# Stick-breaking attention in a hybrid decoder layer: queries on partitions, a scan for the running product, DMA transposes for the weights

## The chip, the cores and the metric

The kernel runs on one core of a Trainium2 chip. The metric is device time of one execution in microseconds (us), taken as the median of three runs. The profile is one further execution; its engines are PE (TensorE matmul; PEld is its weight load), DVE (VectorE), ACT (ScalarE), POOL (GpSimd) and SP (SyncE, which issues most DMAs).

## The reference

One layer: normalise x, project, attend, convolve, gate, project back, and then a feed-forward block with a convolution inside. What the change touches is the attention, with 8 heads of 64 and 1024 positions:

```python
z = jnp.einsum("bhqd,bhkd->bhqk", qb, kb).astype(jnp.float32) * scale
strict = s_idx < t_idx
log_keep = jnp.where(strict, jax.nn.log_sigmoid(-z), 0.0)
later = lax.cumsum(log_keep, axis=3, reverse=True) - log_keep
w = jnp.where(strict, jnp.exp(jax.nn.log_sigmoid(z) + later), 0.0)
outs.append(jnp.einsum("bhqk,bhkd->bhqd", w, vb.astype(jnp.float32)))
```

In words: beta = sigmoid(z). The weight of key s for query t is beta[t,s] times the product of (1 - beta[t,j]) over the keys j between s and t. It is strictly causal. The product can be taken as an exponential of a sum of logarithms, or as a running product that starts at the newest key and runs back.

## The kernel before

Every float32 matrix product is made of three float16 ones: each operand is kept as a high and a low half, and `PASSES` (L35) names the three pairs of halves that are multiplied. A high half is written by an ACT copy, and the low half by a DVE instruction that subtracts the high half from the source. Weights arrive by DMA from SP into `ws` tiles (L103), are squared and summed by ACT (L56), scaled by a power of two and split into `wh` tiles (L86, L87).

The mixer begins with the normalisation of x and the first projections, in an order written out by hand. Then come four calls of `attention(j)`, each for a **pair of heads** (the two heads of a pair lie on partitions 0 to 63 and 64 to 127 of the tiles q and k). Beside each call the function `merge` runs a stream of **projection matmuls**: v for the later positions, q and k of the next pair (`qk_tile`, L200), the convolution branch (`pcc`, `pcx`, `pcb`), and, with the last pair, gates and the first branch outputs. These fill PE while a unit of the attention waits for DVE and ACT. `merge` only sets an order in the source; the final order on each engine is made by a scheduler at build time from dependences and priorities, and is then fixed: each engine takes its instructions in that order and waits when an operand isn't ready.

A pair is cut into twelve **units**. Before the change a unit is one tile of 128 keys (on partitions) by up to 512 queries; widths are 128, 256, 384 and 512, twice each, and 512 four times more, 4608 columns per head in all. The steps of a unit:

- z (L600, six matmuls, three passes for two heads) in PSUM; one buffer of two banks.
- zc: DVE scales z and clamps it, with a mask tile `clamp` on diagonal units (L615, L618).
- sp: ACT takes exp and then ln(1 + .), the softplus (L622, L623); its high half by ACT (L625), its low half by DVE (L626).
- A: PE multiplies sp with a triangle of ones (L600, four matmuls) to sum over the later keys, and after it was read with the other triangle (four more), so that A carries the sum on to the next unit. A takes two banks.
- zc minus A on DVE (L638), exp on ACT (L640): the weights w, with keys on partitions. High half by ACT (L642), low half by DVE (L643).
- o: PE multiplies w with v (L600, six matmuls as wide as the unit, with 64 columns of v as the stationary operand).

All these matmuls are issued by the helper `mm`, so that they have one line, L600. The step o of a unit is written two units after its z.

After the mixer come the branch products (L580), the gates and the out-projection (L859), and the feed-forward block (L1156 and L1048), which the change leaves alone.

Of the kernel before, what the change touches and what calls it, by code (L numbers as in the profile page):

```python
# [37 lines left out]
class Layer:  # L38
# [167 lines left out]
    def build(self):  # L206
# [23 lines left out]
        with ExitStack() as top:  # L230
# [9 lines left out]
            nc.scalar.preload_act_table_set("natural_log_exp_and_others")  # L240
# [7 lines left out]
            self.one = c.tile([P, 1], F32, tag="one", name="one")  # L248
            nc.vector.memset(self.one, 1.0)
            self.cmw = c.tile([P, 4, 3], F32, tag="cmw", name="cmw")  # L250
            self.cfw = c.tile([P, 2 * NFF, 3], F32, tag="cfw", name="cfw")
            tri32 = c.tile([P, P], F32, tag="tri32", name="tri32")
            nc.gpsimd.memset(tri32, 1.0)
            nc.gpsimd.affine_select(tri32, tri32, [[-1, P]], ALU.is_ge, 0.0, base=0, channel_multiplier=1)
            self.tri = c.tile([P, 2, P], F16, tag="tri", name="tri")
            nc.vector.tensor_copy(self.tri[:, 0, :], tri32)
            nc.vector.tensor_scalar(self.tri[:, 1, :], tri32, -1.0, 1.0, ALU.mult, ALU.add)
# [6 lines left out]
    def mixer(self, mid):  # L264
        tc, nc, a = self.tc, self.nc, self.a
        hT = self.hp.tile([P, 2, KD, T], F16, tag="hT", name="hT")
        with ExitStack() as ph1:
# [4 lines left out]
            self.clamp = att.tile([P, 2, NH], F16, tag="clamp", name="clamp")  # L272
            nc.gpsimd.memset(self.clamp, 44.0)
            nc.gpsimd.affine_select(self.clamp[:, :, :P], self.clamp[:, :, :P], [[0, 2], [1, P]], ALU.is_gt,
                                    -30000.0, base=0, channel_multiplier=-1)
# [4 lines left out]
            def qk_tile(j, which):  # L280
# [12 lines left out]
                if which == "k":  # L293
                    cz = self.small(f"cz{j}", keep=True)
                    self.mul(cz[:, 0:1], s["iq"], inv)
                    self.mul(cz[:, 1:2], cz[:, 0:1], cst[:, 0:1])
                    s["cz"] = cz[:, 1:2]
# [293 lines left out]
            def attention(j):  # L591
# [3 lines left out]
                units = [dict(c=c, i=i, off=max(0, i * P - c * NH), top=i == 4 * c + 3, diag=i >= 4 * c,  # L595
                              nm=f"{j}_{c}{i}") for c in range(2) for i in range(4 * c + 3, -1, -1)]
# [5 lines left out]
                def stage1(u):  # L602
                    off, i, c, nm = u["off"], u["i"], u["c"], u["nm"]
                    tsl = ds(c * NH + off, NH - off)
                    z = pat.tile([P, 2, NH], F32, tag="z", name=f"z{nm}")
                    for n, (hk, hq) in enumerate(PASSES):
                        for h in range(2):
                            d = ds(64 * h, 64)
                            with tc.high_priority(10 ** 6):
# [676 lines left out]
```

## Time and profile before

| what | value |
|---|---|
| median of 3 runs | 1367.35 us (1366.69 to 1368.55) |
| profiled execution | 1367.47 us |
| its span, first to last instruction | 1365.7 us |
| PE busy in the span | 1336.1 us |
| DVE busy | 1028.6 us |
| ACT busy | 860.7 us |
| attention stage, first z to last o | about 64 to 411 us |
| moved by DMA | 96.06 MB |

The profiled execution's own time lies 1.8 us above its span. A row of the profile that ends in "x48 | 45.7, 955 | 34.5 <-ACT w L642 34.4" is a group of 48 instructions that were busy for 45.7 us, with a mean of 955 ns; the engine sat idle for 34.5 us just before them, 34.4 of these until an ACT instruction on tile w was done.

### The profile page before, as it was taken

To read this page: it belongs to the slowest core of one execution; us is meant where nothing else is said; L and a number is where in the kernel's file an instruction comes from. 1 tells how busy PE (TensorE), PEld (TensorE's weight loads), DVE (VectorE), ACT (ScalarE), POOL (GpSimd) and SP (SyncE) were. 2 spreads that over 40 slices of the span, in tenths; PEclk is the share of its full clock that TensorE was granted. 3 is DMA by queue.
4 is the path that set the end of the run, shared out by engine and by line. 5 is a ranking of instruction groups with operands and counts; after the bars stand their busy time and mean duration, and the time that the engine had idled before them with its cause. 6 is when DMAs were issued, how large, how long until landed. Compare 5 with 4: busy or idle time off the path is not lost. (4 is left out here: it accounts for less than half of the span.)

```text
span 1365.7 us, 16990 instructions
## 1 busy us (share of the span) xinstructions
PE 1336.1 (98%) x6651; PEld 607.7 (44%) x6651; DVE 1028.6 (75%) x1610; ACT 860.7 (63%) x1204; POOL 34.2 (3%) x52
## 2 busy tenths in 40 slices
PE   6999999999999999999999999999999999999997
PEld 3444444444444444444454444444444444444443
DVE  6667777777775965878788985984894896699855
ACT  6668778787775775666466577652761673476524
POOL 2000000000000000000010000000000000000002
PEclk9999999999999999999999999999999999999999
DMA  7102111101111121351331123122220321313216
GB/s 264 62 1 62 32 31 32 38 25 39 40 31 47 32 62 31 93 185 36 119 124 62 62 62 123 39 87 85 70 78 16 123 62 62 109 45 124 63 46 109
DMA packets 26576, 96.06 MB, mean 70 GB/s; under 512 B 3072, under 2 KB 3200, under 8 KB 26496
## 3 DMA queue, kind: packets, MB, share of 16 engines
q1 hardware_dynamic: 25056, 89.74, 20.3%
q0 software_dynamic: 1440, 5.24, 2.1%
q8 instruction: 52, 0.85, 0.2%
q14 instruction: 28, 0.23, 0.1%
HBM read 86.58 MB, written 8.39 MB: 70 GB/s over the span
## 5 line engine op out<-in xcount | busy, mean ns | idle before, releaser
L1156 PEld LDWEIGHTS <-wh_u 128*128 128x128 f16 x1848 | 178.8, 98 | 217.3 <-issue 3.5
L1048 PE MATMUL pd<-wdh,f 128*128 128x512 f16 (+1 forms) x1068 | 230.3, 377 | 2.8 <-ACT wdh L86 1.2
L1048 PEld LDWEIGHTS <-f 128*128 128x128 f16 x1068 | 104.4, 98 | 127.2 <-issue 4.3
L86 ACT ACTIVATE wh_u<-ws_u,sc 128x1024 f16<-128x1024 f32 (+1 forms) x66 | 64.7, 998 | 102.9 <-DVE sc L78 79.3
L1055 DVE SCALAR_TENSOR_TENSOR yacc<-pd,sd,yacc 128x512 f32<-128x512 f32 (+1 forms) x81 | 58.5, 740 | 72.7 <-PE pd L1048 65.2
L1156 PEld LDWEIGHTS <-wh_g 128*128 128x128 f16 x588 | 56.9, 98 | 68.7 <-issue 0.4
L859 PE MATMUL py<-wh_wo,m 128*128 128x512 f16 x384 | 83.9, 379 | 0.0
L87 DVE SCALAR_TENSOR_TENSOR wh_u<-ws_u,sc,wh_u 128x1024 f16<-128x1024 f32 (+1 forms) x66 | 72.1, 1099 | 9.5 <-ACT wh_u L86 9.4
L643 DVE SCALAR_TENSOR_TENSOR w<-zc,w 128x1024 f16<-128x1024 f32 (+3 forms) x48 | 45.7, 955 | 34.5 <-ACT w L642 34.4
L622 ACT ACTIVATE sp<-zc 128x1024 f32<-128x1024 f32 (+3 forms) x48 | 40.2, 838 | 46.7 <-DVE zc L615 29.1
L600 PE MATMUL A<-sh,tri 128*128 128x512 f16 (+3 forms) x352 | 67.8, 322 | 0.0
L1233 DVE SCALAR_TENSOR_TENSOR ugu<-cgu,cw_g,ugu 128x1023 f32<-128x1023 f32 (+1 forms) x44 | 56.2, 1278 | 11.3 <-ACT ugu L1231 10.9
L1233 DVE SCALAR_TENSOR_TENSOR ua<-cau,cw_a,ua 128x1023 f32<-128x1023 f32 (+1 forms) x44 | 56.1, 1276 | 1.4 <-ACT ua L1231 1.3
L859 PEld LDWEIGHTS <-m 128*128 128x128 f16 x384 | 37.5, 98 | 44.1
L626 DVE TENSOR_TENSOR sh<-sp,sh 128x1024 f16<-128x1024 f32 (+3 forms) x48 | 45.7, 952 | 12.9 <-ACT sh L625 12.7
L640 ACT ACTIVATE zc<-zc 128x1024 f32<-128x1024 f32 (+3 forms) x48 | 40.0, 834 | 15.4 <-DVE zc L638 15.0
L638 DVE SCALAR_TENSOR_TENSOR zc<-A,zc 128x1024 f32<-128x1024 f32 (+3 forms) x48 | 45.5, 949 | 2.3 <-PE A L600 2.3
L56 ACT ACTIVATE jk_u<-ws_u 128x1024 bf16<-128x1024 f32 x44 | 46.4, 1054 | 0.9
L200 PE MATMUL pk<-hT,wh_k 128*128 128x512 f16 x192 | 46.8, 380 | 0.0
L200 PE MATMUL pq<-hT,wh_q 128*128 128x512 f16 x192 | 44.3, 379 | 1.3 <-DVE sc L79 1.3
L623 ACT ACTIVATE sp<-sp,one 128x1024 f32<-128x1024 f32 (+3 forms) x48 | 44.6, 928 | 0.8
L200 PE MATMUL pcb<-hT,wh_cb 128*128 128x512 f16 x192 | 44.8, 379 | 0.0
(620 smaller groups left out, 2606.4 us busy)
## 6 DMA issues: line engine op xcount, KB each, us to landing
ws_u<-w_up_nt SPq DMA_DIRECT2D x44, 512.0 KB, 3.7
ds<-w_down SPq DMA_DIRECT2D x22, 512.0 KB, 6.1
wd<-w_down SPq DMA_DIRECT2D x22, 512.0 KB, 3.7
ws_g<-w_in_nt SPq DMA_DIRECT2D x14, 512.0 KB, 3.6
x<-x SPq DMA_DIRECT2D x8, 512.0 KB, 8.0
ws_wo<-w_out SPq DMA_DIRECT2D x8, 512.0 KB, 7.1
xr<-x SPq DMA_DIRECT2D x8, 512.0 KB, 4.3
out<-x SPq DMA_DIRECT2D x7, 512.0 KB, 2.9
```

The lines of the kernel that those rows point to most:

```text
L56: self.nc.scalar.activation(self.junk(f"jk_{name}"), src, AF.Square, accum_out=acc)
L86: self.nc.scalar.activation(dst[:, 0, :], src, AF.Copy, scale=s)
L87: self.nc.vector.scalar_tensor_tensor(dst[:, 1, :], src, s, dst[:, 0, :], ALU.mult, ALU.subtract)
L200: nc.tensor.matmul(ps, w[:, wi, ds(k * P, P)], hT[:, hi, k, ds(c * NH, NH)], start=n == 0, stop=n == last)
L600: nc.tensor.matmul(out, w, mv, skip_group_check=True, **kw)
L626: nc.vector.tensor_tensor(sh[:, 1, :, off:], sp[:, :, off:], sh[:, 0, :, off:], ALU.subtract)
L643: nc.vector.scalar_tensor_tensor(w[:, 1, :, off:], zc[:, :, off:], 2.0 ** 14, w[:, 0, :, off:], ALU.mult, ALU.subtract)
L859: nc.tensor.matmul(ps, m16[k][:, hi, ds(tt * P, P)], wo[k][:, wi, sl], start=k == 0 and p == 0, stop=k == 7 and p == 2)
L1048: nc.tensor.matmul(pd[nh], f16[g][k][:, hi, ds(tt * P, P)], w[k][:, wi, ds(*part)], start=run is runs[0] and n == 0, stop=run is runs[-1] ...
L1055: nc.vector.scalar_tensor_tensor(y[:, sl], ps, sm[:, 0:1], y[:, sl], ALU.mult, ALU.add)
L1156: nc.tensor.matmul(ps, w[wt][:, wi, ds(wc * NH + k * P, P)], self.block(i, hi, k), start=first and n == 0, stop=n == 3 * KH - 1, skip_grou ...
L1233: nc.vector.scalar_tensor_tensor(u[:, lag:], c[:, :T - lag], sm[:, 2 - lag:3 - lag], u[:, lag:], ALU.mult, ALU.add)
```

## The change

Queries now lie on partitions and keys along the free axis. A unit is one block b of 128 queries by n = 1 to 4 blocks of 128 keys that begin at block i0 (named by pair, b and i0; below "unit 50" is b = 5, i0 = 0). The widths and the count of twelve units a pair stay the same. The newer keys of a query block come first, and C carries the running product to its second unit. The steps:

- z as before with the roles of q and k exchanged, and two buffers of two banks. On diagonal units two `hide` matmuls of 128 columns add -1e30 where the key isn't older than the query.
- ACT takes two sigmoids straight from PSUM: C = sigmoid(-z) and be = sigmoid(z).
- DVE runs a scan over C for each head, backwards in place, so that C becomes the running product; be is multiplied with C shifted by one key.
- High half of w by ACT, low half by DVE, as before.
- wT: one DMA from SP transposes all 128x128 blocks of w (4n of them: two heads, two halves).
- o: per key block six matmuls of 128 columns on wT.

The tiles A, `tri`, `clamp`, `sp` and `sh` are gone. The step o is written three units after z (before: two). `merge` gets 216 in place of 240 as the main stream's total. The ACT table set loaded first is the one with the sigmoid.

```diff
-                    zc = att.tile([P, 2, NH], F32, tag="zc", name=f"zc{nm}", bufs=3)
...
-                    nc.scalar.activation(sp[:, :, off:], zc[:, :, off:], AF.Exp)
-                    nc.scalar.activation(sp[:, :, off:], sp[:, :, off:], AF.Ln, bias=self.one)
...
+                        if u["diag"]:
+                            for h in range(2):
+                                mm(z[:, h, W - P:W], self.hide[:, 1, :], self.hide[:, 0, :], start=False, stop=True)
+                    be = att.tile([P, 2, NH], F32, tag="be", name=f"be{nm}", bufs=3)
+                    C = u["C"] = att.tile([P, 2, NH + 1], F32, tag="C", name=f"C{nm}", bufs=2)
+                    nc.scalar.activation(C[:, :, :W], z[:, :, :W], AF.Sigmoid, scale=s["ncz"])
+                    nc.scalar.activation(be[:, :, :W], z[:, :, :W], AF.Sigmoid, scale=s["cz"])
...
-                    for h in range(2):
-                        for hl in range(2):
-                            mm(A[:, h, off:], self.tri[:, 0, :], sh[:, hl, h, off:],
-                               start=u["top"] and hl == 0, stop=False)
-                    nc.vector.scalar_tensor_tensor(zc[:, :, off:], A[:, :, off:], -1.0, zc[:, :, off:],
-                                                   ALU.mult, ALU.add)
...
+                        nc.vector.tensor_copy(C[:, :, W:], acc["C"][:, :, 0:1])
+                    for h in range(2):
+                        x = C[:, h, :W][:, ::-1]
+                        nc.vector.tensor_tensor_scan(x, x, x, 1.0 if u["diag"] else C[:, h, W:], ALU.mult, ALU.bypass)
+                    nc.vector.tensor_tensor(be[:, :, :m], be[:, :, :m], C[:, :, 1:m + 1], ALU.mult)
+                    w = att.tile([P, 4 * NH], F16, tag="w", name=f"w{nm}", bufs=2)
...
+                    wT = att.tile([P, 16, P], F16, tag="wT", name=f"wT{nm}", bufs=3)
+                    nc.sync.dma_start_transpose(wT[:, :4 * n, :], w[:, :4 * W])
...
+                        for ii in range(n):
+                            i = i0 + ii
+                            for p, (hw, hv) in enumerate(((1, 0), (0, 0), (0, 1))):
+                                for h in range(2):
+                                    mm(o[64 * h:64 * h + 64, ds((b % 4) * P, P)],
+                                       v16[i // 2][:, i % 2, j, 1 + h if hv else 3 * h, :],
+                                       wT[:, (hw * 2 + h) * n + ii, :],
...
-                merge(attention(j), 240, chain(*gens), nf)
+                merge(attention(j), 216, chain(*gens), nf)
```

**PE, third pair.** Before, a stretch in which the sums of a unit (A from sh, the halves of the softplus, and tri, the triangle) stand between z and a projection (pk, for k of the next pair):

```order
L600 MATMUL z_12_2845<-q_1575,k_1734 128x512
L600 LDWEIGHTS tri
L600 MATMUL A_17_2599<-sh_15_2650,tri 128x384
...
L600 MATMUL A_17_2599<-sh_14_2726,tri 128x512
L200 LDWEIGHTS wh_k_0_1894
L200 MATMUL pk_0_2504<-hT,wh_k_0_1894 128x512
...
L600 LDWEIGHTS v_2_113
L600 MATMUL o_17_2701<-w_15_2743,v_2_113 64x384
```

After, the z of unit 54 with its hide matmuls, and further on the o of units 50 and 64 behind a projection (pcb, of the convolution branch):

```order
L596 MATMUL z_54_2694<-k_1802,q_1641 128x256
L596 LDWEIGHTS hide
L596 MATMUL z_54_2694<-hide 128x128
...
L200 MATMUL pcb_1_2352<-hT,wh_cb_0_1633 128x512
L596 LDWEIGHTS v_0_102
L596 MATMUL o_44_2823<-wT_50_2859,v_0_102 64x128
...
L596 MATMUL o_44_2823<-wT_64_2934,v_2_104 64x128
```

No sum is left on PE between z and o, the o of a unit of four key blocks is 24 matmuls of 128 columns, and these wait for wT.

**DVE, third pair.** Before, around unit 14 (zc, sh and w are its clamp, the low half of the softplus and of the weights; sc, cv and wh belong to weights of the projections):

```order
L626 TENSOR_TENSOR sh_14_2726<-sp_14_2723,sh_14_2726 128x1024
L76 TENSOR_SCALAR sc_2487<-pr_2490 128x1
L78 TENSOR_SCALAR sc_2487<-sc_2487 128x1
L79 TENSOR_SCALAR sc_2487<-sc_2487 128x1
L90 TENSOR_TENSOR cv_3097<-g_pre,sc_2487 128x1
L643 SCALAR_TENSOR_TENSOR w_15_2743<-zc_15_2645,w_15_2743 128x2x384
L291 SCALAR_TENSOR_TENSOR q_2344<-pq_1_2425,q_2344 128x512
L618 TENSOR_SCALAR zc_12_2852<-z_12_2845,cz_1866 128x1024
L87 SCALAR_TENSOR_TENSOR wh_cc_0_2495<-ws_cc_0_2182,sc_2487,wh_cc_0_2495 128x1024
L638 SCALAR_TENSOR_TENSOR zc_14_2721<-A_17_2599,zc_14_2721 128x1024
```

After, around unit 50 (L629 is the scan, "x2" one for each head; be is the product; u and o are evictions of projections and of the attention's output):

```order
L624 COPY C_50_2777<-C_54_2704 128x2
L630 TENSOR_TENSOR be_54_2703<-be_54_2703,C_54_2704 128x2x255
L629 SCALAR_TENSOR_TENSOR C_50_2777<-C_50_2777 128x512 x2
L629 SCALAR_TENSOR_TENSOR C_64_2843<-C_64_2843 128x384 x2
L630 TENSOR_TENSOR be_50_2776<-be_50_2776,C_50_2777 128x1024
L530 SCALAR_TENSOR_TENSOR u_1958<-pcx_0_2125,cv_1957,u_1958 128x512
L630 TENSOR_TENSOR be_64_2842<-be_64_2842,C_64_2843 128x2x383
L634 SCALAR_TENSOR_TENSOR w_54_2815<-be_54_2703,w_54_2815 128x512
L658 SCALAR_TENSOR_TENSOR o_2_2430<-o_00_2564,o_2_2430 128x512
L624 COPY C_60_2916<-C_64_2843 128x2
L634 SCALAR_TENSOR_TENSOR w_50_2856<-be_50_2776,w_50_2856 128x1024
```

Four wide passes of a unit became two scans and two wide passes; the scans of the next unit stand ahead of a unit's product and low half.

**SP.** Before, the queue holds only weight loads in this part:

```order
L103 DMA ws_cx_0_2340<-w_in_nt 128x1024
L103 DMA ws_cb_0_2499<-w_in_nt 128x1024
L103 DMA ws_gc_0_2667<-w_in_nt 128x1024
L103 DMA ws_ga_0_2814<-w_in_nt 128x1024
L103 DMA ws_wc_0_2951<-wc 128x1024
```

After, the third pair's transposes stand between them (the second number of a shape is the count of 128x128 blocks):

```order
L103 DMA ws_cx_0_2469<-w_in_nt 128x1024
L637 DMA_TRANSPOSE wT_40_2723<-w_40_2720 128x16x128
L637 DMA_TRANSPOSE wT_54_2818<-w_54_2815 128x8x128
L637 DMA_TRANSPOSE wT_50_2859<-w_50_2856 128x16x128
L637 DMA_TRANSPOSE wT_64_2934<-w_64_2931 128x12x128
L637 DMA_TRANSPOSE wT_60_3008<-w_60_3005 128x16x128
L637 DMA_TRANSPOSE wT_74_3080<-w_74_3077 128x16x128
L103 DMA ws_cb_0_2630<-w_in_nt 128x1024
L637 DMA_TRANSPOSE wT_70_3145<-w_70_3142 128x16x128
```

Each pair adds twelve transposes to SP's queue, and a load behind one of them is issued after it.

More of the change, by code (lines that the diff above doesn't have):

```diff
@@ L670, in stage3 @@
                                                        ALU.mult, ALU.subtract)
-                n = len(units)
-                for k in range(n + 2):
+                n, lag = len(units), 3
+                for k in range(n + lag):
                     if k < n:
```

107 lines of the change are left out of this document (40 added, 67 removed).

## The prediction

> **What bounds the kernel now.** I read the page's first part, then busy time by stage, then the groups with shapes kept apart, the timeline around single units, and the waits. The page says PE; by stage it says so more sharply.
>
> ```profile
> span 1365.7 us, 16990 instructions
> PE 1336.1 (98%) x6651; PEld 607.7 (44%) x6651; DVE 1028.6 (75%) x1610; ACT 860.7 (63%) x1204; POOL 34.2 (3%) x52
> ```
> ```profile
> 64.00:411.00 347.00, 347.00 (x1984) 151.03 (x1984) 249.14 (x382) 265.83 (x355) 0.00 (x0) 1.00 0.12 34
> ```
>
> The second fence is the attention stage, from the first z to the last o (columns: PE, PEld, DVE, ACT, POOL busy, clock, DMA share, GB/s). PE has no idle time in 347 us, DVE stands at 72%, ACT at 77%, DMA at 12%, and the clock is full. So matmul time taken out here comes off the end, as long as nothing else becomes late.
>
> **PE's work, removed and added.** A matmul's duration contains its pipeline; what it costs is the distance to the next start. Groups first, then pairs of timeline rows: six o matmuls of one unit and what starts behind them, four widths, then z and A.
>
> ```profile
> L859 PE MATMUL py<-wh_wo,m 128*128 128x512 f16 x384 | 83.9, 379 | 0.0
> L600 PE MATMUL A<-sh,tri 128*128 128x512 f16 x160 | 40.2, 379 | 0.0
> L600 PE MATMUL A<-sh,tri 128*128 128x384 f16 x64 | 13.6, 327 | 0.0
> L600 PE MATMUL A<-sh,tri 128*128 128x256 f16 x64 | 10.5, 274 | 0.0
> L600 PE MATMUL A<-sh,tri 128*128 128x128 f16 x64 | 6.8, 221 | 0.0
> ```
> ```profile
> 76.62 0.36 PE L600 MATMUL o<-w,v 128*64 128x128 f16 x6
> 76.92 0.28 PE L600 MATMUL A<-sh,tri 128*128 128x256 f16 x1
> ...
> 92.54 0.68 PE L600 MATMUL o<-w,v 128*64 128x384 f16 x6
> 93.15 0.39 PE L600 MATMUL A<-sh,tri 128*128 128x512 f16 x1
> ...
> 98.17 0.40 PE L600 MATMUL A<-sh,tri 128*128 128x128 f16 x4
> 98.40 0.38 PE L343 MATMUL pv<-wh_v,hT 128*128 128x512 f16 x1
> ...
> 99.39 0.84 PE L600 MATMUL o<-w,v 128*64 128x512 f16 x6
> 100.16 0.82 PE L600 MATMUL z<-q,k 64*128 64x512 f16 x6
> ...
> 113.32 0.52 PE L600 MATMUL o<-w,v 128*64 128x256 f16 x6
> 113.77 0.39 PE L200 MATMUL pq<-hT,wh_q 128*128 128x512 f16 x1
> ```
>
> The out-projection's row gives 83.9/384 = 0.2185 us for 512 columns at full rate, the fifth pair row 0.23/4 = 0.0575 us for 128. The A matmuls go: 160 x 0.2185 + 64 x (0.164 + 0.109 + 0.0575) = 56.2 us (their own busy column, 71.1, counts tails that lie over other matmuls; it is the far bound). The o matmuls become 864 of 128 columns in place of 288 wider ones. Six of 128 take 0.30 us, 0.050 each; the widths 512, 384, 256 take 0.128, 0.102, 0.075. Before: 144 x 0.128 + 48 x (0.102 + 0.075 + 0.050) = 29.4 us; after: 864 x 0.050 = 43.2 us, so 13.8 more (20 if each cost the 0.0575 of A). The 64 hide matmuls add 64 x 0.0575 = 3.7 us. The z matmuls keep counts and widths and cost nothing new. Net on PE: -56.2 + 13.8 + 3.7 = **-38.7 us**. The profiled execution took 1367.47 us (span 1365.7), the median is 1367.35, so PE alone would give 1328.8.
>
> **ACT.** Per unit five passes become three. The groups of the stage:
>
> ```profile
> L640 ACT ACTIVATE zc<-zc 128x1024 f32<-128x1024 f32 x24 | 25.2, 1050 | 12.1 <-DVE zc L638 11.8
> L623 ACT ACTIVATE sp<-sp,one 128x1024 f32<-128x1024 f32 x24 | 27.4, 1141 | 0.3
> ```
>
> A sigmoid with a per-partition scale is priced between these, 1.05 to 1.14 us at full width. ACT loses two passes of five; I cost it at nothing, since PE hides it before and after. The dropped table load, the smaller setup on POOL and DVE, and the projection matmuls that now stand behind the attention instead of inside it also count nothing: PE's total is the same wherever they stand. The weight loads on SP's queue now stand behind transposes; they run two tiles ahead, and a late one costs at most its landing (below, 3.7 us) once.
>
> **DVE, and the end of each head pair.** Removed per unit: three passes over two heads (the clamp out of PSUM, the low half of the softplus, the subtraction of A). Added: two scans and one product. Prices by width, the other groups in the queue, and three neighbours on the timeline:
>
> ```profile
> L643 DVE SCALAR_TENSOR_TENSOR w<-zc,w 128x1024 f16<-128x1024 f32 x24 | 29.4, 1223 | 24.0 <-ACT w L642 23.9
> L643 DVE SCALAR_TENSOR_TENSOR w<-zc,w 128x768 f16<-128x768 f32 x8 | 7.6, 954 | 2.5 <-ACT w L642 2.4
> L643 DVE SCALAR_TENSOR_TENSOR w<-zc,w 128x512 f16<-128x512 f32 x8 | 5.5, 688 | 7.2 <-ACT w L642 7.2
> L643 DVE SCALAR_TENSOR_TENSOR w<-zc,w 128x256 f16<-128x256 f32 x8 | 3.3, 418 | 0.8 <-ACT w L642 0.8
> L87 DVE SCALAR_TENSOR_TENSOR wh_cb<-ws_cb,sc,wh_cb 128x1024 f16<-128x1024 f32 x4 | 5.1, 1283 | 5.9 <-ACT wh_cb L86 5.9
> L535 DVE SCALAR_TENSOR_TENSOR u<-pcx,cv,u 128x512 f32<-128x512 f32 x8 | 5.9, 743 | 0.6 <-PE pr L74 0.6
> ```
> ```profile
> 100.25 0.14 DVE L79 TENSOR_SCALAR sc<-sc 128x1 int32<-128x1 int32 x1
> ...
> 106.94 1.28 DVE L615 SCALAR_TENSOR_TENSOR zc<-z,cz,clamp 128x1024 f32<-128x1024 f32 x1
> 108.14 1.28 DVE L87 SCALAR_TENSOR_TENSOR wh_cb<-ws_cb,sc,wh_cb 128x1024 f16<-128x1024 f32 x1
> 109.33 0.68 DVE L643 SCALAR_TENSOR_TENSOR w<-zc,w 128x512 f16<-128x512 f32 x1
> ```
>
> Instructions of 1.28 us start 1.20 apart: 0.08 of each lies over the next. The trace has no scan. The least a scan of 512 can cost is the 512 row, 0.688 us; each product needs the one before it, which no row here does, so I bound it above by twice the elements, the 1024 row, 1.223 us, and take that end because of this dependence. [...]
>
> Now the third pair, from the scan of unit 20 to the low half of unit 70: 60 instructions in DVE's order. Scans: 12 x 1.223 + 4 x 0.954 + 2 x 0.688 + 2 x 0.418 = 20.7 us; the ten products and ten low halves 10.3 each; two weight halves and two convolution lags at 1.28, three evictions at 0.74, one of o at 0.69, twelve tiny ones at 0.14: 9.7. Sum 51.0, less 60 x 0.08, is 46.2 us. Ahead of it a sigmoid of 768 (about 0.9) must finish, behind it the transpose must land. In the same stretch PE has 143 projection matmuls (31.2), 30 z of 512 at 0.125 (3.8), 18 narrower z (1.4), 192 o (9.6), hide and tiny ones (0.8): 46.8 us, and then it reaches the o of unit 70, which waits.
>
> ```profile
> ws_u<-w_up_nt SPq DMA_DIRECT2D x44, 512.0 KB, 3.7
> ...
> out<-o SPq DMA_DIRECT2D x2, 256.0 KB, 2.6
> ```
> ```profile
> 109.44 0.33 SPq L103 DMA_DIRECT2D ws_cx<-w_in_nt  x1
> ```
>
> A unit's transpose of four blocks moves 512 KB. No row shows a transposing DMA. The low bound is a plain load of this size, 3.7 us; the far bound is sixteen 128x128 blocks each landing by itself at 2.6 us, 41.6; in between, sixteen issues of 0.33 us and one landing, 7.9. I take 3.7, the row of the same size, and keep the others. Then the o of unit 70 is due 0.9 + 46.2 + 3.7 = 50.8 us after the stretch began, and PE is there after 46.8: it waits 4.0 us. The fourth pair has the same order (4.0); the second has 157 projection matmuls and 51.0 against 49.9 (1.1); the first 168 and 51.8 against 53.3 (none). Together about **+9 to 10 us**, and the sum is 1328.8 + 10 = **1339**.
>
> The new waits, and what stands behind them: a transpose waits on SP for DVE's w, with weight loads behind it; an o waits on PE for its transpose, with projections behind it; ACT's copy into w waits for the landing of two units before, with the next sigmoids behind it, and PE's z needs their PSUM. For the last, two full units take DVE 2 x 4 x 1.223 = 9.8 us, of which copy and low half use 2.3, so a landing under 7.5 us costs nothing; the forecast's 3.7 lies below, the 7.9 just above.
>
> [...]
>
> **Rivals.** *The scan runs at one element a cycle.* Scans then cost 11.9 instead of 20.7 us a pair, no pair is late, and the time is 1329. For it: two-input passes here do about one element per ns; against it, the dependence.
>
> *Transposes go block by block.* A pair holds 144 blocks and leaves about 50 us between its first transpose and its last o (the 46.8 us above and about 7 of z and projections ahead of them, less 4 until the first w is done), so from 50/144 = 0.35 us a block the queue, not PE, sets the pace. SP's issue of 0.33 lies just under it, a landing of 2.6 far over it. At the geometric middle, 0.93, a pair needs 134 us, and the time is 1329 + 4 x 84 = 1665; even 0.42 a block already eats the gain. [...] For it: the DMA's own small pieces must be scattered over all partitions. Against it: DMA is 12% busy, so throughput as such is there.
>
> *The handovers between ACT and DVE come to the path.* The low half of w waits for ACT's copy in both kernels:
>
> ```profile
> DVE w L643 <- ACT w L642: 34.4, 26, 2.7
> ```
>
> Today PE covers these 34.4 us, 8.6 a pair. With DVE at 46 of 51 us there is no cover left: if all return, pairs are late by 7.1, 9.7, 12.6 and 12.6, together 42, and 1328.8 + 42 = 1371. From 9.7 us of lateness a pair the change loses. Against it: an engine that is itself behind finds ACT's copies done.
>
> **How the numbers follow.** Forecast 0.41 (own range 1325 to 1357: below by the far bound of A, above by the transpose at 7.9, which makes three pairs 4.2 and one 2.7 later); fast scan 0.12; handovers 0.15, split 0.03, 0.05 and 0.07 into faster, same and slower; block by block 0.32, all slower. A measurement of this kernel tells 0.2% from no change, so: faster 0.56, same 0.05, slower 0.39. The range runs from 1325 to 1490 (a block price of 0.63 us), which leaves out half of the block case and a little below.
>
> **What would show it.** Right: z, o and hide rows with the starts above; scans near 1.2 us at 512; transposes landing in 3 to 5 us; PE idle only at the last o of a pair, a few us; attention stage plus displaced projections 29 us shorter. Wrong: PE idle at every o with a transposing DMA as releaser, or a landing time that grows with the number of blocks and SP's queue full (block by block); DVE idle behind ACT's copy (handovers); scans near 0.7 us. Also wrong, if o pieces of 128 columns start farther apart than 0.06 us.

## The result, and the profile after

| | median | range | runs |
|---|---|---|---|
| before | 1368.31 us | 1365.98 to 1369.84 | 17 |
| after | 1370.07 us | 1366.92 to 1375.47 | 17 |

The ratio is 1.0018, with a 95% interval of 1.0008 to 1.0028: within the 0.2% that the prediction calls no change, and at most 0.3% slower. The forecast was 1339, 31 us less than measured. The profiled execution took 1369.98 us, its span is 1368.3.

PE's work fell much as forecast, the time did not. First the page, then the stage from the first z to the last o and the stretch behind it (columns: PE, PEld, DVE, ACT, POOL busy, granted clock, DMA share, GB/s), then the row of the first projection that needs the attention's output (its start is the first figure after the durations):

```profile
PE 1308.5 (96%) x6939; PEld 606.8 (44%) x6939; DVE 1025.1 (75%) x1628; ACT 786.8 (58%) x1107; POOL 33.0 (2%) x50
```
```profile
64.00:411.00 347.00, 317.43 (x2261) 149.12 (x2262) 245.50 (x390) 192.54 (x257) 0.00 (x0) 0.95 0.43 89
411.00:470.00 59.00, 57.44 (x272) 26.04 (x271) 42.91 (x66) 34.64 (x48) 0.00 (x0) 1.00 0.16 45
```
```profile
L575 PE MATMUL pywa<-o,wh_wa x192: 377/379/379, 466.5 to 541.5; 128*128 128x512 f16 x192
```

And the last two of these views for the kernel before:

```profile
411.00:470.00 59.00, 57.70 (x271) 26.17 (x272) 44.92 (x60) 37.29 (x51) 0.00 (x0) 1.00 0.15 45
```
```profile
L580 PE MATMUL pywa<-o,wh_wa x192: 376/379/379, 464.3 to 539.3; 128*128 128x512 f16 x192
```

Two things are new in the stage (the same view of the kernel before stands in the prediction). PE, which had not one idle microsecond in 347, is idle for 347 - 317.4 = 29.6. And the clock, 1.00 before, is 0.95: in the trace's clock record it falls to half seven times, 37.5 us in all, which is 18.7 us of lost work. The first wa projection starts at 466.5 in place of 464.3, and from there on the two kernels run alike (901.4 and 901.8 us to the end of the span).

The prices of the new operations, from the groups of the changed kernel (first fence) and its DMA issues (second: median from issue to landing):

```profile
L629 DVE TENSOR_TENSOR_SCAN C<-C 128x512 f32<-128x512 f32 x48 | 57.9, 1246 | 1.0 <-ACT C L614 0.5
L634 DVE SCALAR_TENSOR_TENSOR w<-be,w 128x1024 f16<-128x1024 f32 x24 | 29.2, 1218 | 5.6 <-ACT w L633 5.6
```
```profile
wT<-w SPq DMA_TRANSPOSE x48, 4.3
```

The scan of 512 took 1.246 us, just above the upper end of its bounds (1.223). The transpose landed after 4.3 in the median and 6.2 at most, under the 7.9 of sixteen issues and one landing and far from the 41.6 of sixteen landings, so the rival that prices them by the block did not come. The waits of the stage (engine, line, releaser: us in total, times, longest):

```profile
PE o L596 <- DMA wT<-w: 22.9, 16, 3.3
PE z L596 <- ACT be L615: 3.4, 3, 1.6
PE o L596 <- DVE o L658: 1.8, 2, 1.3
...
DVE w L634 <- ACT w L633: 6.0, 9, 1.5
```

PE waits for turned weights 16 times, not at the four ends of pairs. The forecast's rival of the handovers did not come: DVE's wait for ACT's copy fell from 34.4 us to 6.0. That this rival's sum, 1371, is near the measured time is chance. Where DVE stands is seen in windows of 16 us over the third pair (columns as above):

```profile
240.00:256.00 16.00, 15.90 (x117) 6.64 (x115) 15.97 (x26) 13.48 (x18) 0.00 (x0) 0.98 0.65 129
256.00:272.00 16.00, 13.01 (x119) 6.31 (x119) 15.89 (x19) 10.24 (x10) 0.00 (x0) 1.00 0.37 72
272.00:288.00 16.00, 11.16 (x97) 6.12 (x97) 12.49 (x20) 7.01 (x9) 0.00 (x0) 0.80 0.76 127
288.00:304.00 16.00, 16.00 (x96) 7.39 (x95) 4.15 (x11) 4.98 (x9) 0.00 (x0) 0.99 0.28 74
```

For 32 us DVE is busy with hardly a gap, then PE starves (11.2 of 16) at a clock of 0.80, and right behind it PE has almost nothing but projections while DVE is at a quarter. A share of 75% over the span hides a stretch at 100% beside one at 26%.

### The profile page after: what moved, and what is told of

It reads as the page before. It is cut to its first block, busy times and chain, and to the rows that moved or that the text cites. A ratio compares the mean times of both kernels' runs of the same rounds, so it can differ in the third digit from the quotient of the medians.

```text
span 1368.3 us, 17653 instructions
## 1 busy us (share of the span) xinstructions
PE 1308.5 (96%) x6939; PEld 606.8 (44%) x6939; DVE 1025.1 (75%) x1628; ACT 786.8 (58%) x1107; POOL 33.0 (2%) x50
## 5 line engine op out<-in xcount | busy, mean ns | idle before, releaser
L629 DVE TENSOR_TENSOR_SCAN C<-C 128x512 f32<-128x512 f32 (+3 forms) x96 | 87.5, 960 | 7.8 <-ACT C L614 7.3
L1143 PEld LDWEIGHTS <-wh_g 128*128 128x128 f16 x588 | 56.9, 98 | 68.6 <-issue 0.3
L596 PE MATMUL o<-wT,v 128*64 128x128 f16 x864 | 44.0, 234 | 24.7 <-DMA wT<-w 22.9
L633 ACT ACTIVATE w<-be 128x1024 f16<-128x1024 f32 (+3 forms) x48 | 40.1, 844 | 46.7 <-DVE be L630 28.1
L1220 DVE SCALAR_TENSOR_TENSOR ugu<-cgu,cw_g,ugu 128x1023 f32<-128x1023 f32 (+1 forms) x44 | 56.2, 1277 | 11.6 <-ACT ugu L1218 11.2
L846 PEld LDWEIGHTS <-m 128*128 128x128 f16 x384 | 37.5, 98 | 44.1
L596 PEld LDWEIGHTS <-v 128*64 128x64 f16 x864 | 32.1, 116 | 46.7 <-issue 41.0
L614 ACT ACTIVATE C<-z,cz 128x1024 f32<-128x1024 f32 (+3 forms) x48 | 41.4, 894 | 18.4 <-PE z L596 14.5
L634 DVE SCALAR_TENSOR_TENSOR w<-be,w 128x1024 f16<-128x1024 f32 (+3 forms) x48 | 45.4, 950 | 6.0 <-ACT w L633 6.0
L200 PE MATMUL pcc<-hT,wh_cc 128*128 128x512 f16 x192 | 47.6, 402 | 0.0
L200 PE MATMUL pcx<-hT,wh_cx 128*128 128x512 f16 x192 | 46.6, 395 | 0.0
L200 PE MATMUL pk<-hT,wh_k 128*128 128x512 f16 x192 | 43.4, 379 | 1.4 <-DVE q L285 1.4
```

The lines of the kernel that those rows point to most:

```text
L200: nc.tensor.matmul(ps, w[:, wi, ds(k * P, P)], hT[:, hi, k, ds(c * NH, NH)], start=n == 0, stop=n == last)
L596: nc.tensor.matmul(out, w, mv, skip_group_check=True, **kw)
L629: nc.vector.tensor_tensor_scan(x, x, x, 1.0 if u["diag"] else C[:, h, W:], ALU.mult, ALU.bypass)
L634: nc.vector.scalar_tensor_tensor(wv_[:, 1], be[:, :, :W], 2.0 ** 14, wv_[:, 0], ALU.mult, ALU.subtract)
L846: nc.tensor.matmul(ps, m16[k][:, hi, ds(tt * P, P)], wo[k][:, wi, sl], start=k == 0 and p == 0, stop=k == 7 and p == 2)
L1143: nc.tensor.matmul(ps, w[wt][:, wi, ds(wc * NH + k * P, P)], self.block(i, hi, k), start=first and n == 0, stop=n == 3 * KH - 1, skip_grou ...
```

## The experiments

The runs were taken in batches of five rounds beside the kernel before, each batch on one chip (e1 to e4, e5 to e8, e9 to e12, e13 and e14), so runs of different batches are compared by their ratios. The theories of the first wave were these. **W**: the transposes are late. **S**: z and o matmuls, which now alternate one by one on PE, cost turns and the clock. **D**: the scans make DVE the bound. After the first wave, **T**: DVE's work is crowded into a part of each pair, and its sum there sets the end; **L**: the time from one unit's z to its turned weights counts.

The table takes each stage apart. Stage: first wa projection less 64 us. Idle: the two stage windows' length less PE's busy time. Half clock: half the length of the low stretches in the clock record. Rest: what remains, PE's work at full clock. Stage, idle, half clock and rest are of the profiled execution, the median of all.

| run | median us | ratio to before, 95% | stage | PE idle | half clock | rest |
|---|---|---|---|---|---|---|
| before | 1368.31 | 1 | 400.3 | 1.3 | 0 | 399.0 |
| after | 1370.07 | 1.0018 (1.0008 to 1.0028) | 402.5 | 31.1 | 18.7 | 352.7 |
| e1_zfirst | 1368.68 | 1.0007 (0.9994 to 1.0019) | 395.8 | 40.1 | 13.7 | 342.0 |
| e2_noturn | 1358.79 | 0.9931 (0.9919 to 0.9944) | 390.3 | 22.0 | 13.7 | 354.6 |
| e3_onepass | 1336.36 | 0.9761 (0.9744 to 0.9779) | 369.3 | 9.9 | 5.1 | 354.3 |
| e5_halfscan | 1347.47 | 0.9850 (0.9836 to 0.9863) | 376.5 | 12.9 | 6.8 | 356.8 |
| e6_onepass_z | 1332.10 | 0.9736 (0.9723 to 0.9750) | 363.7 | 19.9 | 1.7 | 342.1 |
| e7_o_behind | 1356.71 | 0.9907 (0.9892 to 0.9922) | 388.2 | 18.4 | 11.9 | 357.9 |
| e8_zo_behind | 1335.67 | 0.9765 (0.9752 to 0.9779) | 366.1 | 10.6 | 5.1 | 350.4 |
| e11_paced_onepass | 1323.58 | 0.9679 (0.9663 to 0.9694) | 356.2 | 4.6 | 0 | 351.6 |
| e14_paced_noturn | 1327.98 | 0.9702 (0.9688 to 0.9715) | 360.1 | 9.7 | 3.4 | 347.0 |
| e13_double_z | 1386.87 | 1.0136 (1.0122 to 1.0150) | 419.7 | 38.0 | 17.0 | 364.7 |

### First wave: alternation, transposes, scans

```diff
-                    with tc.high_priority(10 ** 6):
+                    with tc.high_priority(2 * 10 ** 6):
                         for n_, (hk, hq) in enumerate(PASSES):
```

> The z matmuls get a higher priority than the o, so that on PE the z of a unit stands in one piece instead of alternating with o matmul by matmul (turns between z and o in PE's order: 25 instead of 97); nothing else is edited. Theory S (the alternation costs a drain at each turn and brings the clock down) expects 1345 to 1352 us, z back near its 32 us of busy time and at most two of the nine dips of the granted clock. Theory W (the transposes are late, and each wait of an o costs its own time and half-rate time after it) expects 1360 to 1372, with the 16 waits of o for transposes still there. Theory D (the scans make DVE the bound) expects 1362 or more.

Measured 1368.68 us, which is D's and W's range and not S's. PE's wait for turned weights in this run (22.9 us, 16 times, in the changed kernel):

```profile
PE o L596 <- DMA wT<-w: 26.8, 21, 4.0
```

The rest of the stage fell by 10.7 us for 72 turns fewer, 0.15 us a turn, so the alternation does cost PE. But idle time rose by 9.0: what PE saves, it waits. S is true as a price and false as the cause.

```diff
-                    wT = att.tile([P, 16, P], F16, tag="wT", name=f"wT{nm}", bufs=3)
-                    nc.sync.dma_start_transpose(wT[:, :4 * n, :], w[:, :4 * W])
-                    u["wT"] = wT
+                    u["wT"] = w.rearrange("p (g s) -> p g s", s=P)
```

(w gets four buffers in place of two.)

> The DMA transposes are left out: the o matmuls read the weights unturned, so the output is not the reference's. DVE, ACT and the scans do all they did. W expects about 1335 us: the waits of PE on transposes (22.9 us) gone, and with them most of the half-rate clock. S expects no gain, 1365 or more, since z and o alternate as before (110 turns). D expects 1362 or more, with the o now waiting on DVE's w instead of on the DMA.

Measured 1358.79 us. From 1.0018 to 0.9931 are 12 us, a third of what W expected. The wait stayed and took another name:

```profile
PE o L596 <- DVE w L634: 18.3, 13, 2.7
```

So W falls as the main cause: a releaser that is last in a chain is not the one that makes the chain long.

```diff
-                        nc.vector.tensor_tensor_scan(x, x, x, 1.0 if u["diag"] else C[:, h, W:], ALU.mult, ALU.bypass)
+                        nc.vector.tensor_tensor(x, x, x, ALU.mult)
```

> Each scan is replaced by a one-pass VectorE product of the same tile, so the running product is left out of the computation. D expects about 1340 us: some 25 us less of DVE in the stage, and PE never late. W expects about 1355, since the w come earlier but the transposes still land 4 us after them. S expects 1365 or more (111 turns as before).

Measured 1336.36 us, near D's 1340. One product of 512 takes 0.686 us in place of the scan's 1.246, and over the execution DVE has 1025.1 - 987.8 = 37.3 us less; the time fell by 0.0257 x 1368 = 35. Microsecond for microsecond, in a kernel whose DVE is at 75%. PE's waits for weights:

```profile
PE o L596 <- DMA wT<-w: 4.0, 4, 2.3
```

The transposes are still there, and they are waited for 4 times and not 16.

```diff
                     o = acc["o"]
-                    with tc.high_priority(10 ** 6):
+                    with tc.high_priority(0):
...
-                        with tc.high_priority():
-                            stage3(units[k - lag])
+                        stage3(units[k - lag])
```

> The o matmuls lose every high priority, so that they stand at least 18.7 us (46.5 on average) behind their z in PE's order instead of about 15, and turn with z 30 times instead of 97; nothing is computed otherwise. W expects 1335 to 1340 us: transposes land long before they are asked for, no waits, clock 1.00. S expects about 1345, from the fewer turns. D expects 1362 or more.

Measured 1434.76 us, ratio 1.0486 (1.0468 to 1.0505), above every expectation. PE hardly waits (2.6 us between 64 and 470 us), and the clock is 1.00, yet the groups of o and of one projection read

```profile
L596 PE MATMUL o<-wT,v 128*64 128x128 f16 x864 | 132.4, 235 | 0.0
...
L200 PE MATMUL pcb<-hT,wh_cb 128*128 128x512 f16 x192 | 67.0, 387 | 0.0
```

against 44.0 and 44.5 in the changed kernel, with nearly the same mean duration of one (234 and 390 ns there). Without the priority the o matmuls were dealt out singly and in pairs between projections, some thousand changes between o and projection in PE's order in place of 53. In the changed kernel's blocks two neighbouring o of the two heads start 3 to 4 ns apart in most pairs, and one pair follows another after 55 to 56 ns. Between projections a pair holds PE for 0.18 us here (124.69 to 124.87), and between z a lone one holds it as long (97.28 to 97.46 in e3). The stage's rest is 459 us, 107 more than in the changed kernel, for 933 more changes: 0.11 us a change, near what e1 priced. The run says nothing on late o; e7 does that part alone.

### Second wave: half the scans, and the order

```diff
-                        nc.vector.tensor_tensor_scan(x, x, x, 1.0 if u["diag"] else C[:, h, W:], ALU.mult, ALU.bypass)
+                        if h == 0:
+                            nc.vector.tensor_tensor_scan(x, x, x, 1.0 if u["diag"] else C[:, h, W:], ALU.mult, ALU.bypass)
+                        else:
+                            nc.vector.tensor_tensor(x, x, x, ALU.mult)
```

> Only the scan of the first head is kept; that of the second head is replaced by a one-pass VectorE product, so the running product is left out for half of the heads. Theory T (the sum of DVE's work in the dense part of each pair sets the end, so time follows DVE's work in proportion) expects half of what replacing both scans gave: 1350 to 1357 us. Theory L (what counts is how long one unit takes from z to its turned weights) expects under a third of it, since only the second scan of each unit is shorter: 1360 or more. If the gain came from a threshold that is crossed, such as clock dips that vanish all at once, the time is near one of the ends, under 1345 or over 1362.

Measured 1347.47 us, a little under T's range: from 1.0018, half the scans give 0.0168 and all of them 0.0257, so two thirds of the gain for half of the work. L is out. In proportion it is not quite: the first half saves the clock dips as well (18.7 to 6.8 us).

e6 is e3 and e1 together.

> Both scans replaced by one-pass products (the running product is left out) and z at the higher priority, so that z and o hardly alternate. Theory T expects that without the scans PE is the bound, so the turns that were free before now show: 97 turns less some 25 at about 0.16 us each are 11 us, which gives 1323 to 1330. If the alternation costs PE nothing, the time stays at 1336.

Measured 1332.10 us, between the two expectations. The rest fell by 12.2 us, for 85 turns fewer (0.14 each), as reckoned; idle rose from 9.9 to 19.9. Even with one-pass products PE is close enough to DVE that most of what it saves turns into waiting.

```diff
+                def behind():
+                    return tc.issue_after(next(i for i in reversed(nc.cur_bb.bb.instructions)
+                                               if i.engine == mybir.EngineType.PE))
...
                     o = acc["o"]
-                    with tc.high_priority(10 ** 6):
+                    with behind(), tc.high_priority(10 ** 6):
```

> The o matmuls of a unit are issued behind the projections that stand ahead of them in the program's text, and still in one block (high priority kept): they stand 49 us behind their z on average instead of 15, without being split as in the run with late o. z is not moved. Nothing is computed otherwise. T and L both expect that PE no longer waits for weights: first wa projection at about 430 us instead of 466.5 and 1330 to 1340 in all, with a clock of 1.00. If the late o of the earlier run lost its time for another reason than the split (buffers held too long, the tail after the last unit), the time is above 1380 here too.

Measured 1356.71 us: some 15 us better than the changed kernel, half or less of the 30 to 40 that both theories expected. The waits of o for weights are gone, and others stand there:

```profile
PE z L596 <- ACT be L619: 7.5, 5, 3.0
PE o L596 <- DVE o L662: 4.0, 2, 2.0
```

DVE is hardly crowded any more here (of the stage's windows of 16 us one, in the first pair, is still full). In the third pair it is at 86% and 85% in the two windows in which it was full, and at 72% and 71% in the next two:

```profile
240.00:256.00 16.00, 15.12 (x152) 7.39 (x150) 13.79 (x22) 8.72 (x11) 0.00 (x0) 1.00 0.46 97
256.00:272.00 16.00, 16.00 (x106) 6.83 (x103) 13.64 (x23) 12.17 (x19) 0.00 (x0) 1.00 0.36 75
```

z, which runs ahead as before, waits for the sigmoid `be` that frees its PSUM buffer. Before each of the five waits of z, ACT had itself waited with that sigmoid, until DVE's low half of w freed a buffer of be:

```profile
ACT be L619 <- DVE w L638: 25.3, 24, 2.6
```

So PE can be late over another chain although DVE's work is spread, and T as it stood doesn't explain this run. Moving the one that waits is not enough.

e8 gives the z group the same line as well:

```diff
-                    with tc.high_priority(10 ** 6):
+                    with behind(), tc.high_priority(10 ** 6):
                         for n_, (hk, hq) in enumerate(PASSES):
```

> z and o are both issued behind the projections that stand ahead of them in the program's text, each in one block. The attention of a pair is thereby spread over its projections instead of standing in the first two thirds of it; o stands 20 us behind its z on average. Nothing is computed otherwise, and every scan stays. T expects that DVE's work of a pair now has the whole pair's time, some 76 us, so hardly any wait, clock 1.00, and 1320 to 1330 us. L expects only part of it, 1345 to 1360, since o still stands as near as 8 us behind some z. D in its strict form (DVE cannot do more in the stage, wherever the work stands) expects 1362 or more.

Measured 1335.67 us, 0.9765 (0.9752 to 0.9779) of before, with every scan and every transpose in it and nothing left out: the fastest of the kernels that compute all of the reference. The stage, PE's wait for transposes, and the windows where the third pair was crowded:

```profile
64.00:411.00 347.00, 336.40 (x2423) 151.60 (x2422) 267.45 (x430) 208.01 (x281) 0.00 (x0) 0.99 0.44 93
```
```profile
PE o L596 <- DMA wT<-w: 1.6, 1, 1.6
```
```profile
224.00:240.00 16.00, 16.00 (x147) 7.92 (x146) 10.69 (x21) 7.45 (x12) 0.00 (x0) 1.00 0.30 68
240.00:256.00 16.00, 15.29 (x102) 6.19 (x99) 13.90 (x26) 11.63 (x20) 0.00 (x0) 1.00 0.44 93
256.00:272.00 16.00, 15.96 (x117) 7.39 (x116) 13.33 (x22) 11.72 (x16) 0.00 (x0) 1.00 0.56 112
272.00:288.00 16.00, 16.00 (x113) 6.89 (x110) 11.78 (x18) 8.66 (x12) 0.00 (x0) 1.00 0.42 92
```

DVE does the same work at 67% to 87% in each window, not at 100% and then 26%, and PE waits once for a transpose. Same instructions, another order, 34 us: this rules out L and the strict form of D, and shows that the lost time lay in the order. T comes nearest without being met: it expected 1320 to 1330 us and a clock of 1.00, and 10.6 us of idle time and 5.1 of half clock are left. e8 also moves z, and turns between z and o fall from 97 to 32, so what the spread of DVE's work gives by itself is not measured alone.

### Third wave: is it the order alone?

e9 is the kernel before with the same two edits.

> The kernel before, with z and o issued behind the projections that stand ahead of them in the program's text, as in the run of the changed kernel that did this. Nothing is computed otherwise. Theory T says that the kernel before had no wait to win back: PE was busy for 347.0 of 347.0 us of the stage, covered by the triangular sums. It expects 1355 to 1372 us, a change of under 1%. If it falls to 1340 or lower, the gain of the spread order has nothing to do with the scans and the change is worth nothing of it.

Measured 1407.63 us, ratio 1.0293 (1.0278 to 1.0309): the spread order makes the kernel before slower, by more than T allowed for. Up to 411 us little is lost (PE is busy for 343.5 of 347.0 us); behind that, and above all from 441 to 481 us, the last units stand with hardly a projection beside them:

```profile
411.00:470.00 59.00, 39.40 (x184) 14.93 (x181) 43.53 (x48) 51.02 (x57) 0.00 (x0) 0.81 0.05 15
```

So the gain of e8 is not one that any kernel gets from this order. That the kernel before could keep its attention crowded because its triangular sums kept PE at work there is likely, but no run tests it.

```diff
-                    nc.vector.tensor_tensor(be[:, :, :m], be[:, :, :m], C[:, :, 1:m + 1], ALU.mult)
+                    nc.gpsimd.tensor_tensor(be[:, :, :m], be[:, :, :m], C[:, :, 1:m + 1], ALU.mult)
```

> The changed kernel in its own order, with the product of sigmoid and running product on GpSimd instead of VectorE; nothing is left out, and the scans stay. It takes 48 products, some 45 us, off DVE. T expects 1333 to 1345 us, like the run without scans, if GpSimd needs under 2.5 us for a product. If it needs 5 us or more, or slows DVE beside it, the units come later and the time is 1365 or more. L expects no gain, since the chain of a unit gets no shorter.

Measured 1382.98 us, ratio 1.0108 (1.0091 to 1.0125): the branch in which GpSimd slows DVE.

```profile
L630 POOL TENSOR_TENSOR be<-be,C 128x1024 f32<-128x1024 f32 (+4 forms) x48 | 86.3, 1797 | 235.5 <-DVE C L629 137.9 <-DVE sc L79 67.5 <-ACT be L615 24.9
```
```profile
L629 DVE TENSOR_TENSOR_SCAN C<-C 128x512 f32<-128x512 f32 x48 | 74.6, 1596 | 1.5 <-ACT C L614 0.9
L634 DVE SCALAR_TENSOR_TENSOR w<-be,w 128x1024 f16<-128x1024 f32 x24 | 36.3, 1513 | 3.7 <-ACT w L633 3.7
```

The product took 1.80 us on average over its widths on GpSimd (an estimated 2.4 at 1024, from 86.3 us over 36800 columns if a column costs the same at every width), within the bound of 2.5. But the scans beside it went from 1.246 to 1.596 us and the low halves from 1.218 to 1.513, and over the execution DVE was busy for 1035.5 us, with 45 us of work taken away, against 1025.1. It is no test of T, since DVE's time did not fall.

e11 is e8 and e3 together, e12 is e8 and e10 together.

> The spread order (z and o behind the projections ahead of them), and both scans replaced by one-pass products, so that the running product is left out. T expects that the scan's price is covered once the work is spread: 1328 to 1336 us, where the same edit gave 34 us in the crowded order. If the scans still cost in proportion, the time is 1310 or less.

> The spread order, and the product on GpSimd; nothing is left out. T expects next to nothing beyond the spread order, 1328 to 1337 us, since DVE is no longer the bound. If GpSimd is slow, a unit's chain grows and o waits: 1340 or more.

Measured 1323.58 and 1338.09 us (e12's ratio 0.9782, 0.9767 to 0.9796), below the 1328 to 1336 that T expected of e11 and just above its 1328 to 1337 for e12. In the spread order the scans cost 12 us, where they cost 35 in the crowded one; T expected 0 to 8. Two thirds of their price is covered, and the last third is 6.0 us of idle and 5.1 of half clock. The product on GpSimd neither helps nor hurts beyond the noise.

e13 is e1 with each group of z issued twice:

```diff
-                        for n_, (hk, hq) in enumerate(PASSES):
+                        for n_, (hk, hq) in enumerate(PASSES + PASSES):
...
-                                   start=n_ == 0, stop=n_ == 2 and not u["diag"])
+                                   start=n_ in (0, 3), stop=n_ == 5 and not u["diag"])
```

> The run with z at the higher priority, and each group of six z matmuls issued twice (the second overwrites the first, so nothing changes in what is computed). That adds 288 z matmuls, 28 us of PE work at the starts that z showed. If PE is not the bound in the dense part of a pair (theory T), the added work falls into waits that are there anyway, and the time is 1366 to 1382 us, with fewer dips of the clock. If the lost time is not PE idling behind DVE, but PE work that is slower than I reckoned, nearly all of it shows: 1390 to 1400.

Measured 1386.87 us, 18 us above e1 and between the two. In the profiled executions, which lie 21 us apart, the rest rose by 22.7 us against e1, and the idle time fell by only 2.1. The waits point to why T's expectation failed (first of e1, then of this run):

```profile
ACT C L614 <- PE z L596: 6.8, 5, 3.0
```
```profile
ACT C L614 <- PE z L596: 24.5, 11, 4.7
```

z stands ahead of the sigmoids and of DVE. Work that is put there delays the very chain that PE waits for, and so it covers next to nothing. e8 suggests that projections, which stand outside that chain, do fill the idle time.

e14 is e8 and e2 together.

> The spread order without the DMA transposes: the o read the weights unturned, so the output is not the reference's. In the crowded order leaving them out gave 11 us. T expects that a landing of 4 us is covered once the o stand 20 us behind their z: 1331 to 1337 us against 1336. If transposes cost by themselves (their traffic, the queue of SP), the time is 1325 or less.

Measured 1327.98 us, between the two: the transposes cost 8 us in the spread order and 12 in the crowded one. Leaving them out also takes most of the 32 turns between z and o out of PE's order (2 are left). Of the 6.0 us that the stage is shorter, 3.4 are rest, 1.7 half clock and 0.9 idle time, so hardly any of it is waiting for a landing; why the end of the kernel gains a little more stays open.

## Why the prediction was wrong

By its own steps, with the third pair as its example:

**PE's work: right side, somewhat small.** Forecast -38.7 us; the rest went from 399.0 to 352.7, that is -46.3. Added up over the traces from each matmul's start to the next, with idle time and half clock taken out, the parts are: A 56.9 us gone (forecast 56.2), o +3.3 (31.3 to 34.6; forecast +13.8), z +3.7 (29.1 to 32.8; forecast nothing), hide +4.9 (3.7), projections and tiny ones -1.4. So the mis-sized term is the o, 0.040 us each and not 0.050: the six whose price the forecast took end in a change of shape, and in a block of 24 that change is shared (24 in 0.86 us in the last row of the fence below). The z costs more, since it turns with o 97 times and not 33; the forecast left that out ("The z matmuls keep counts and widths and cost nothing new").

**The scan: right.** Taken at 1.223, measured 1.246; a one-pass product of the same width takes 0.686 (e3), so the scan costs 1.8 times as much. The prediction took the upper end because each product needs the one before it; the rows show the price, not its cause.

**The transposes: right.** Taken at 3.7, measured 4.3 in the median of all 48. The landing does grow with the blocks, which the prediction named as a sign of the rival: the medians are 2.5, 3.1, 3.7 and 4.6 us for 4, 8, 12 and 16. But that is some 0.17 us for each further block, half of the 0.35 from which the queue would set the pace, and SP stood waiting for `w` for 137.1 us ahead of the transposes. A plain load of 512 KB (`ws_u`) landed after 3.6 in the same execution. The small pieces that the rival named are there, 73728 packets of 256 B, 128 for each of the 576 blocks. SP's instruction for one transpose took 1.7 us in the median, not 0.33.

**DVE's stretch: right in length.** Forecast 46.2 us from the scan of unit 20 to the low half of unit 70. First and last of it on the timeline:

```profile
235.25 4.04 DVE L629 TENSOR_TENSOR_SCAN C<-C 128x384 f32<-128x384 f32 x4 [0.63 <-ACT C L614]
...
277.67 1.22 DVE L634 SCALAR_TENSOR_TENSOR w<-be,w 128x1024 f16<-128x1024 f32 x1
...
282.30 1.23 DVE L634 SCALAR_TENSOR_TENSOR w<-be,w 128x1024 f16<-128x1024 f32 x1 [1.49 <-ACT w L633]
```

283.53 - 235.25 = 48.3 us, 1.5 of them a wait for ACT.

**The wait of PE: this step failed.** The prediction said: "the o of unit 70 is due 0.9 + 46.2 + 3.7 = 50.8 us after the stretch began, and PE is there after 46.8: it waits 4.0 us", and nothing at the others. PE's timeline from the end of unit 20's z on, idle time in brackets:

```profile
230.46 3.83 PE L200 MATMUL pcc<-hT,wh_cc 128*128 128x512 f16 x17
...
235.00 0.47 PE L596 MATMUL o<-wT,v 128*64 128x128 f16 x10 [0.41 <-DMA wT<-w]
...
237.06 0.40 PE L596 MATMUL z<-k,q 64*128 64x128 f16 x6 [1.60 <-ACT be L615]
...
260.74 0.30 PE L596 MATMUL o<-wT,v 128*64 128x128 f16 x4 [1.29 <-DVE o L658]
261.29 0.61 PE L596 MATMUL z<-k,q 64*128 64x512 f16 x4 [0.24 <-ACT be L615]
...
273.10 0.69 PE L596 MATMUL o<-wT,v 128*64 128x128 f16 x18 [2.56 <-DMA wT<-w]
...
281.17 1.14 PE L596 MATMUL o<-wT,v 128*64 128x128 f16 x24 [2.52 <-DMA wT<-w]
283.53 1.49 PE L596 MATMUL o<-wT,v 128*64 128x128 f16 x24 [1.22 <-DMA wT<-w]
284.95 6.83 PE L200 MATMUL pq<-hT,wh_q 128*128 128x512 f16 x23
291.72 0.86 PE L596 MATMUL o<-wT,v 128*64 128x128 f16 x24
```

The idle times sum to 9.8 us, and the o of unit 70, at 291.72, is the one that does not wait: 23 projections stand ahead of it. The forecast set the two totals against each other at the end of the pair alone. PE's order is fixed, so its idle time up to any point is the greatest lateness on the way, not the last. With the prediction's own figures, one o earlier, at unit 74: 23 projections (5.0 us) and one o (1.2) fewer lie behind PE, so it is there after 40.6; the low half of unit 74 stands 3.1 us of DVE's work ahead of that of unit 70 (277.67 to 282.30, less the wait of 1.49; by the prediction's prices it is 3.1 too), so it is due after 47.7. The wait is 7.1, not 4.0. The rows for this stood in the order of the instructions.

The rest of the 9.8 is mostly a term that the forecast put at nothing, the weight loads ("a late one costs at most its landing (below, 3.7 us) once"). On ACT the sum of squares of a weight tile stands ahead of the sigmoids of unit 20, and the tile came late:

```profile
233.28 1.06 ACT L56 ACTIVATE jk_cc<-ws_cc 128x1024 bf16<-128x1024 f32 x1 [3.50 <-DMA ws_cc<-w_in_nt]
...
234.34 1.89 ACT L614 ACTIVATE C<-z,cz 128x768 f32<-128x768 f32 x2
```

The z were done when the projections began at 230.46, the sigmoids began at 234.34: DVE's stretch started 3.9 us late. At the same place of the fourth pair ACT waited 2.84 us for such a load. From its first scan DVE took 43.6 us to the low half of unit 74 (43.1 by the forecast's figures), the landing is 4.3 for 3.7, and the half clock (0.50 in the clock record from 237.2 to 240.6 us and again from 281.6) held PE back by an estimated 2 us: 7.1 + 3.9 + 0.5 + 0.6 - 2 is about 10, and 9.8 were measured.

**The clock: a term that was missing.** The sum took the clock as 1.00. It lost 18.7 us in the stage; in the window of 272 to 288 the granted clock was 0.80.

The stage's sum, which must close since the rest is a remainder, gives the sizes: idle 29.8 more than before and not 9.5 (+20.3), clock 18.7 and not 0 (+18.7), PE's work 7.6 less (-7.6): +31.4 to the forecast of 1339 gives 1370. Both misses go together: e3 and e5 take work off DVE, e8 spreads it, and idle time and half clock fall in all three. e7 spreads it too and keeps 18.4 us of idle time and 11.9 of half clock, so the crowd on DVE is shown as a cause, but not as the only one. Why the clock falls stays open. The forecast weighed a gain of 38.7 us against a wait a third of the real one and against no loss of clock.

## What to carry to other kernels

When work is taken off the bound engine, ask what it covered: the second engine's busy share over the stage says little, its busy share in windows of a few units says where it may be the bound. Check lateness at every wait in the fixed order and not at the end of a stretch, since the greatest one counts. And when a change makes an engine dense in a part of a stage, move the order before the operation is blamed: here the same instructions, spread, took 34 us less. Such a move has to be tried: it cost the kernel before 40 us (e9).

## What the runs showed of the hardware

**In these runs the clock fell to half after short waits, and without any.** In the run with one-pass products (e3) PE was busy without a gap from 80 to 128 us. Three windows of it:

```profile
92.00:96.00 4.00, 4.00 (x22) 1.68 (x19) 3.74 (x7) 1.78 (x3) 0.00 (x0) 1.00 0.67 128
96.00:100.00 4.00, 4.00 (x23) 1.63 (x24) 1.23 (x1) 1.22 (x2) 0.00 (x0) 0.74 0.34 66
100.00:104.00 4.00, 4.00 (x25) 1.85 (x22) 3.22 (x7) 3.54 (x4) 0.00 (x0) 0.50 0.68 131
```

What stands there are z and o in turns, nearly all one by one, from 94.1 to 99.5 us; on the timeline a z begins every 0.44 to 0.5 us, until the clock falls at 97.9 and the next z takes 0.60 us in place of 0.39:

```profile
97.46 0.39 PE L596 MATMUL z<-k,q 64*128 64x512 f16 x1
97.78 0.24 PE L596 MATMUL o<-wT,v 128*64 128x128 f16 x1
97.95 0.60 PE L596 MATMUL z<-k,q 64*128 64x512 f16 x1
```

In the changed kernel's stage the longest gap of PE was 3.3 us and every other one under 2.7, and each low stretch lasted 3.4 or 6.8 us in the clock record. In the 7 us ahead of two of them, at 100.7 and 332.8 us, no gap was longer than 0.34 and 1.06. What brings the clock down is not shown by these runs. Changes between matmuls alone did not do it in e4: 986 between o and projections, at a clock of 1.00.

**A change between differently shaped matmuls cost PE 0.11 to 0.15 us here** (10.7 us for 72 turns of z and o in e1, 12.2 for 85 in e6, 107 for 933 changes between o and projection in e4), and it is seen in starts, not in the duration of one: in the changed kernel a projection starts 0.216 us behind a projection, a z or an o behind one 0.31 (medians). The rows give z as `64*128`, o as `128*64` and a projection as `128*128`; why the change costs this much is not shown.

**GpSimd beside DVE**: in e10 the product on GpSimd made VectorE's scans of 512 28% longer (1246 to 1596 ns) and its two-input passes of 1024 24% longer (1218 to 1513). Why they are longer, these rows don't show.
